# Mixer A's value phase: the sums of a group's weight blocks tied behind the last group's end, and the first rotary tables behind the last sums

## The chip, the cores and the metric

The kernel runs on one core of one Trainium2 chip. A core has TensorE (PE in the profile, with PEld for its weight loads), VectorE (DVE), ScalarE (ACT), GpSimd (POOL) and SyncE (SP), which run side by side and wait for one another by semaphores, and 16 DMA engines. The metric is the device time of one execution in microseconds (us), the median of several.

## The reference

A two-layer encoder over 512 positions of width 1024 in fp32. Layer 0 mixes its tokens with mixer A, layer 1 with mixer B (latent attention), and each mixer is followed by a squared-ReLU MLP. The change touches mixer A, which is, shortened:

```python
def dilated_mixer(h, w_qkv, q_gain, k_gain, w_o):
    qkv = (h @ w_qkv).reshape(B, S, 3, N_GROUPS, A_HEADS, A_HEAD_DIM)
    for g, (window, dil) in enumerate(DIL_CONFIGS):      # 3 groups, 8 heads of 128
        q = rope(rms_norm(qkv[:, :, 0, g], q_gain[g]), S)
        k = rope(rms_norm(qkv[:, :, 1, g], k_gain[g]), S)
        v = qkv[:, :, 2, g]
        o, lse = dilated_group(q, k, v, window, dil)
    wts = softmax(stack(lses), axis=0)
    o = wts[0] * outs[0] + wts[1] * outs[1] + wts[2] * outs[2]
    return o.reshape(B, S, A_WIDTH) @ w_o
```

In words: the normed input h (512 x 1024) is projected to queries, keys and values for three dilation groups, queries and keys are normed and rotated, each group attends in its own window, and the three outputs are merged by their softmax denominators and projected by w_o.

## The kernel before, in words

Matmuls run in fp32r, an fp32 form that keeps fewer bits. So each fp32 operand x is split into a high part (ScalarE copies x to fp32r, "whi" for weights) and a low part (VectorE subtracts it from x, "wlo"), and a product is three matmuls: high by high, high by low, low by high. TensorE waits for both parts, so behind every weight block stand one ScalarE and one VectorE instruction.

The value phase (`v_phase`) computes the values of heads 0 to 5 of each group g = 0, 1, 2 by a block scheme with seven products in place of eight. Rows of h are in two halves, and the weight of a group is cut in 2 x 2 blocks b11, b12, b21, b22 of 512 x 384 that SyncE's queue loads into a ring of six buffers ("wq"). The products are numbered as in the code, and run in the order 2, 1, 5, 3, 6, 7, 4. Products 2, 1, 3 take blocks themselves; 5 takes bT = b11 + b12; 6 takes bT after + b22; 4 takes it after + b21 as well; 7 takes b3 = b12 + b22. All of these sums are VectorE's, two instructions of 128 x 768 each (`add_block`, L349, which shows as "bT<-b,b", "bT<-bT,b" and, for b3, "b<-b,b"). Each product's weights are split in two parts (L421 ScalarE, L422 VectorE; "whi" and "wlo" are rings of four buffers, so a split must wait until TensorE has done with the block four splits back), then 24 matmuls of 384 columns go to each of two PSUM banks (L436). `put` adds a product into the output: the first product of a chain is copied by ScalarE (L453), a later one added or subtracted by VectorE (L455, "vo<-vo,sc"), whereupon TensorE may write the next product of that chain. Chain "a" holds products 1, 6, 7 and 4 in the two banks "sc", so TensorE begins product 7 in a bank when VectorE's subtraction of product 6 has read it.

The first rotary tables (`tables`, L271 and L274, four VectorE instructions) multiply cosines and sines with the gains of group 0's queries and keys. Before, they sit in group 1 behind the put "add".

Behind the value phase come, for four pairs of heads (b = 0 to 3), the query and key projections ("acc<-whi,hT", "acc<-wlo,hT", L191), scores ("sc<-qkT", L591 to L602), the merge of the groups (two small matmuls "scm", L657 and L682, with a chain of small VectorE work between and the scaling of all P, L688, behind), and the products of P with the values (`pv`): transposes of P (L125), copies to pT (L698 VectorE, L705 ScalarE), matmuls L712 and L716 into "sco", and the copy to oT (L718). In the last block there is no next projection, and the output projection ("acc<-whi,hT" with 512 columns) of the heads that are done is mixed in.

The order on each engine is set by a scheduler that lists the instructions by a timeline that it works out itself, over all engines at once. `tc.issue_after(x)` makes what is written under it be listed only behind instruction x. In this change both ends of every tie are VectorE instructions, so the order of VectorE's list keeps it.

Of the kernel before, what the change touches and what calls it, by code (L numbers as in the profile page):

```python
# [10 lines left out]
F32 = mybir.dt.float32  # L11
# [3 lines left out]
ALU = mybir.AluOpType  # L15
# [8 lines left out]
NG = 3  # L24
# [64 lines left out]
def encoder_kernel(ctx: ExitStack, tc: tile.TileContext, x, norm_mix, norm_ffn, a_w_qkv, a_q_gain, a_k_gain,  # L89
# [3 lines left out]
    V, A, G, PE = nc.vector, nc.scalar, nc.gpsimd, nc.tensor  # L93
    uid = [0]
    marks = {}

    def nm(s):
        uid[0] += 1
        return f"{s}_{uid[0]}"
# [167 lines left out]
    def tables(g, gqk, cos, sin):  # L267

        for t in range(2):
            gb = gqk[:, t].rearrange("p (f d) -> p f d", f=2).unsqueeze(1).broadcast_to([P, NT, 2, 64])  # L270
            V.tensor_tensor(cosg[g][:, :, t].rearrange("p r (f d) -> p r f d", f=2),  # L271
                            cos.rearrange("p (r d) -> p r d", r=NT).unsqueeze(2).broadcast_to([P, NT, 2, 64]), gb,
                            op=ALU.mult)
            V.tensor_tensor(sing[g][:, :, t].rearrange("p r (f d) -> p r f d", f=2),  # L274
                            sin.rearrange("p (r f d) -> p r f d", r=NT, f=2), gb, op=ALU.mult)
# [46 lines left out]
    def v_phase(vp):  # L322
# [17 lines left out]
        def block(g, ki, ni, name):  # L340
            t = vp.tile([P, 4, VH], F32, tag="wq", name=nm(name), bufs=6)
            for u in range(2):
                nc.sync.dma_start(t[:, 2 * u:2 * u + 2], wblk(g, ki, ni, u))
            return t

        def add_block(t, x, y):
            for u in range(2):
                us = slice(2 * u, 2 * u + 2)
                V.tensor_tensor(t[:, us], x[:, us], y[:, us], op=ALU.add)  # L349

        def load_x(r):
            for hf in range(2):
# [2 lines left out]
        b11, b21, bT, b12, b22 = {}, {}, {}, {}, {}  # L355
# [62 lines left out]
        def split_w(x):  # L418
            hi = wp.tile([P, 2, 512], F32R, tag="whi", name=nm("whi"))[:, :, :VH]
            lo = wp.tile([P, 2, 512], F32R, tag="wlo", name=nm("wlo"))[:, :, :VH]  # L420
            A.activation(hi, x, AF.Copy)  # L421
            V.tensor_tensor(lo, x, hi.bitcast(F32), op=ALU.subtract)  # L422
            return hi, lo

        def split(p, w, u):
            parts[p, u] = split_w(w[:, 2 * u:2 * u + 2])

        def product(p, w, banks, first, u, t):
            if (p, u) not in parts:
                split(p, w, u)  # L430
            hi, lo = parts[p, u]
            for j in range(2):
                k = 2 * u + j
                ah, al = A_OF[p](k, 0, t), A_OF[p](k, 1, t)
                for i_, (lt, rt) in enumerate(((ah, hi), (ah, lo), (al, hi))):
                    PE.matmul(banks[t][:, :VH], lhsT=lt, rhs=rt[:, j], start=(first and k == 0 and i_ == 0),  # L436
                              stop=(k == 3 and i_ == 2), skip_group_check=True)

        def both(p, w, banks, first):
            for u, t in ((0, 0), (0, 1), (1, 0), (1, 1)):  # L440
                product(p, w, banks, first, u, t)

        def new_banks(chain):
            pl, tg = {"a": (sc_p, "sc"), "b": (tp_p, "tp"), "d": (acc_p, "acc")}[chain]
            return [pl.tile([P, 512], F32, tag=tg, name=nm(tg)) for _ in range(2)]

        def put(g, i, n, how, banks, last):

            o = vo[:, 2 * i + n]
            for t in range(2):  # L450
                acc = banks[t][:, :VH]
                if how == "set":
                    A.activation(o[:, t], acc, AF.Copy)  # L453
                else:
                    marks["put"] = V.tensor_tensor(o[:, t], o[:, t], acc,  # L455
                                                   op=ALU.add if how == "add" else ALU.subtract).ins
                if last:

                    nc.gpsimd.dma_start(vall[g].rearrange("(m r) d -> m r d", r=NT)
                                        [:, 2 * i + t, VH * n:VH * n + VH], o[:, t])  # L460

        def piece(g, ba):

            bb = new_banks("b")
            both(5, bT[g], bb, True)
            put(g, 1, 1, "set", bb, False)
            add_block(bT[g], bT[g], b22[g])
            both(3, b22[g], bb, False)
            put(g, 0, 1, "set", bb, False)
            b3 = vp.tile([P, 4, VH], F32, tag="h32", name=nm("b3"))  # L470
            add_block(b3, b12[g], b22[g])
            both(6, bT[g], ba, False)
            put(g, 0, 1, "sub", ba, True)
            add_block(bT[g], bT[g], b21[g])
            both(7, b3, ba, False)
            put(g, 1, 1, "sub", ba, True)
            both(4, bT[g], ba, False)
            put(g, 1, 0, "set", ba, True)

        def sum_tile():  # L480
            return vp.tile([P, 4, VH], F32, tag="wq", name=nm("bT"), bufs=6)
# [44 lines left out]
        for i in range(2):  # L526
            split_s(2, dif[:, 1, i], i)
        piece(0, ba)

        rot = vp.tile([P, D], F32, tag="xn", name="rot", bufs=2)  # L530
        nc.sync.dma_start(rot[:, 0:C_M1 - C_KEEP], consts[:, C_KEEP:C_M1])
        g0 = rot[:, 768:1024].rearrange("p (t d) -> p t d", t=2)
        load_gains(0, g0)
        for g in range(1, NG):
            b21[g] = block(g, 1, 0, "b21")
            b11[g] = block(g, 0, 0, "b11")
            b12[g] = block(g, 0, 1, "b12")
            b22[g] = block(g, 1, 1, "b22")
            bT[g] = sum_tile()
            parts = {}  # L540
            bd, ba = new_banks("d"), new_banks("a")
            both(2, b21[g], bd, True)
            put(g, 0, 0, "set", bd, False)
            both(1, b11[g], ba, True)
            put(g, 0, 0, "add", ba, True)
            if g == 1:

                with tc.issue_after(marks["put"]):
                    tables(0, g0, rot[:, 0:256], rot[:, 256:768])
            add_block(bT[g], b11[g], b12[g])  # L550
            piece(g, ba)

    ap0 = tc.tile_pool(name="ap0", bufs=1, reuse_waits="tile")
    a0 = ap0.__enter__()
    cosg, sing = ([a0.tile([P, NT, 2, DH], F32, name=n)] for n in ("cosg0", "sing0"))
    with tc.tile_pool(name="vph", bufs=1, reuse_waits="tile") as vp:
        v_phase(vp)
# [701 lines left out]
```

## Time and profile before

| | us |
|---|---|
| median of 3 runs | 1404.27 |
| lowest and highest | 1403.55, 1405.62 |
| profiled execution | 1403.76 |
| its span, first to last instruction | 1402.0 |
| TensorE busy | 1371.6 |
| VectorE busy | 940.0 |
| ScalarE busy | 801.0 |
| GpSimd busy | 224.0 |

The span is what the trace covers; the profiled execution's own time is 1.8 us longer. TensorE's mean granted clock is 0.999. In the trace the value phase's first matmul of L436 stands at 11.1 us and its last at 123.9 us, and the transposes of P run from 236.7 to 497.5 us. A pause of TensorE shows in brackets behind the instruction that follows it, with the instruction that ended it.

### The profile page before, as it was taken

To read this page: it belongs to the slowest core of one execution; us is meant where nothing else is said; L and a number is where in the kernel's file an instruction comes from. 1 tells how busy PE (TensorE), PEld (TensorE's weight loads), DVE (VectorE), ACT (ScalarE), POOL (GpSimd) and SP (SyncE) were. 2 spreads that over 40 slices of the span, in tenths; PEclk is the share of its full clock that TensorE was granted. 3 is DMA by queue.
4 is the path that set the end of the run, shared out by engine and by line. 5 is a ranking of instruction groups with operands and counts; after the bars stand their busy time and mean duration, and the time that the engine had idled before them with its cause. 6 is when DMAs were issued, how large, how long until landed. Compare 5 with 4: busy or idle time off the path is not lost.

```text
span 1402.0 us, 18979 instructions
## 1 busy us (share of the span) xinstructions
PE 1371.6 (98%) x6852; PEld 1163.6 (83%) x6852; DVE 940.0 (67%) x1498; ACT 801.0 (57%) x1643; POOL 224.0 (16%) x240
## 2 busy tenths in 40 slices
PE   7999999999999999999999999999999999999998
PEld 6999887888889989888888878777769888888887
DVE  6886777787788744464655768788745465574747
ACT  6544778687786624453536455777534553644543
POOL 1110212121122001020200204433201020020101
PEclk9999999999999999999999999999999999999999
DMA  9535553655555539486583944211116668493835
GB/s 309 170 134 163 134 130 97 164 131 125 143 130 120 158 106 271 135 186 174 123 237 87 234 96 95 61 31 31 46 46 189 172 131 230 98 234 119 198 88 120
DMA packets 171774, 197.83 MB, mean 141 GB/s; under 512 B 59104, under 2 KB 109024, under 8 KB 171680
## 3 DMA queue, kind: packets, MB, share of 16 engines
q1 hardware_dynamic: 152496, 157.55, 37.7%
q0 software_dynamic: 19184, 39.07, 15.5%
q8 instruction: 54, 0.88, 0.3%
q14 instruction: 40, 0.33, 0.1%
HBM read 176.13 MB, written 7.86 MB: 131 GB/s over the span
## 4 chain that ended last, share of the span: by engine, by line
PE 80%; DVE 7%; DMA 4%; issue 4%; ACT 3%; POOL 1%; SPq 0%; ACTq 0%; DVEq 0%; POOLq 0%
PE acc L191 49%; PE sc L877 9%; PE tp L877 6%; PE sc L436 3%; PE tp L125 2%; DMA wqs<-in_ffn_w_dram 2%; PE acc L1170 1%; DVE wlo L820 1%; PE sc L1064 1%; DMA xT<-t 1%; PE acc L1146 1%; PE tp L436 1%; PE sc L602 1%; PE sco L716 1%; PE sco L712 1%
## 5 line engine op out<-in xcount | busy, mean ns | idle before, releaser
L191 PE MATMUL acc<-whi,hT 128*128 128x512 f32 (+2 forms) x1208 | 377.2, 388 | 1.9 <-ACT hT L761 1.0
L191 PE MATMUL acc<-hT_f,whi 128*128 128x512 f32 (+1 forms) x1152 | 317.5, 366 | 0.0
L159 DVE TENSOR_TENSOR wlo<-raw,whi 128x1024 fp32r<-128x1024 f32 (+3 forms) x146 | 172.8, 1188 | 169.3 <-ACT whi L158 168.8
L191 PEld LDWEIGHTS acc<-whi,hT 128*128 128x128 f32 x1208 | 224.4, 188 | 42.7 <-ACT hT L761 1.7
L158 ACT ACTIVATE whi<-raw 128x1024 fp32r<-128x1024 f32 (+3 forms) x146 | 149.7, 1029 | 159.6 <-PE acc L191 74.8
L191 PEld LDWEIGHTS acc<-hT_f,whi 128*128 128x128 f32 x1152 | 207.9, 189 | 34.9
L191 PE MATMUL acc<-wlo,hT 128*128 128x512 f32 (+2 forms) x604 | 232.9, 386 | 0.4 <-DVE wlo L159 0.4
L820 DVE TENSOR_TENSOR wlo<-wqs,whi 128x1024 fp32r<-128x1024 f32 x112 | 137.7, 1231 | 114.0 <-ACT whi L819 113.9
L819 ACT ACTIVATE whi<-wqs 128x1024 fp32r<-128x1024 f32 x112 | 118.3, 1060 | 162.0 <-PE acc L191 66.2
L191 PE MATMUL acc<-hT_f,wlo 128*128 128x512 f32 (+1 forms) x576 | 204.1, 366 | 0.0
L877 PE MATMUL sc<-whi,asp 128*128 128x512 f32 x512 | 165.1, 390 | 1.0 <-DVE resid L851 1.0
L805 POOL DMA_DIRECT2D wqs<-in_ffn_w_dram x64 | 77.7, 1347 | 539.7 <-DVE wlo L820 358.1
L191 PEld LDWEIGHTS acc<-wlo,hT 128*128 128x128 f32 x604 | 113.7, 188 | 20.1 <-DVE wlo L159 1.0
L191 PEld LDWEIGHTS acc<-hT_f,wlo 128*128 128x128 f32 x576 | 108.3, 189 | 17.3
L877 PEld LDWEIGHTS sc<-whi,asp 128*128 128x128 f32 x512 | 96.2, 188 | 21.6 <-issue 1.8
L877 PE MATMUL tp<-whi,asp 128*128 128x512 f32 x352 | 112.1, 390 | 0.9 <-DVE resid L851 0.9
L133 POOL TENSOR_TENSOR qrs<-rs_v,nhalf 128x4 f32<-128x4 f32 x48 | 64.6, 1348 | 265.0 <-DVE rs_v L130 241.8
L877 PE MATMUL sc<-wlo,asp 128*128 128x512 f32 x256 | 99.7, 390 | 0.0
L307 ACT ACTIVATE qkT<-xT 128x1024 uint16<-128x1024 uint16 x48 | 56.5, 1181 | 39.5 <-DMA xT<-t 39.4
L877 PEld LDWEIGHTS tp<-whi,asp 128*128 128x128 f32 x352 | 66.1, 188 | 15.0 <-DVE resid L851 1.3
L877 PE MATMUL tp<-wlo,asp 128*128 128x512 f32 x176 | 68.2, 390 | 0.0
L138 ACT ACTIVATE junk<-acc 128x128 f32<-128x128 f32 x192 | 52.3, 273 | 12.3 <-PE acc L191 8.7
(236 smaller groups left out, 2186.8 us busy)
## 6 DMA issues: line engine op xcount, KB each, us to landing
wqs<-in_ffn_w_dram SPq DMA_DIRECT2D x80, 512.0 KB, 5.0
raw<-in_ffn_w_dram SPq DMA_DIRECT2D x64, 512.0 KB, 4.6
wqs<-in_ffn_w_dram POOLq DMA_DIRECT2D x64, 512.0 KB, 7.2
raw<-in_a_w_qkv_dram SPq DMA_DIRECT2D x96, 256.0 KB, 3.2
b<-in_a_w_qkv_dram SPq DMA_DIRECT2D x24, 384.0 KB, 5.7
vall<-vo POOLq DMA_DIRECT2D x24, 192.0 KB, 2.3
raw<-in_a_w_o_dram SPq DMA_DIRECT2D x8, 512.0 KB, 4.1
raw<-in_b_w_o_dram SPq DMA_DIRECT2D x8, 512.0 KB, 3.8
```

What stands on the lines that cost most here:

```text
L125: return PE.transpose(o, i, ident)
L133: G.tensor_tensor(out, v[:, :n], nhalf[:, :n], op=ALU.pow)
L138: A.activation(junk, x, AF.Square, scale=1.0 / math.sqrt(dim), accum_out=out)
L158: A.activation(hi[:, :nk, :n], raw[:, :nk, :n], AF.Copy)
L159: V.tensor_tensor(lo[:, :nk, :n], raw[:, :nk, :n], hi[:, :nk, :n].bitcast(F32), op=ALU.subtract)
L191: last = PE.matmul(accs[o][:, oc], lhsT=lt, rhs=rt, start=(kt == 0 and p_i == 0 and hv == 0), stop=(kt == total - 1 and p_i == 2), skip_gr ...
L307: A.activation(dst, xT.rearrange("p (h c) t -> p c t h", h=2), AF.Copy)
L436: PE.matmul(banks[t][:, :VH], lhsT=lt, rhs=rt[:, j], start=(first and k == 0 and i_ == 0), stop=(k == 3 and i_ == 2), skip_group_check=True)
L805: marks["sum"] = nc.gpsimd.dma_start(t, src, accum_op=ALU.add).ins
L819: A.activation(hi, x, AF.Copy)
L820: V.tensor_tensor(lo, x, hi.bitcast(F32), op=ALU.subtract)
L877: PE.matmul(bk[t], lhsT=lt, rhs=rt[:, j], start=(first and k == 0 and i_ == 0), stop=(k == 3 and i_ == 2), skip_group_check=True)
```

## The change

`add_block` returns its last instruction, and the splits and puts are marked, so that others can be tied behind them. For groups 1 and 2, the first sums (bT = b11 + b12) are issued after the last group's second subtraction of product 7 ("minus") and after the last split of product 2; the sums b3 are issued after the sums bT + b22. The first rotary tables are issued after the sums bT + b21 of the last group. No computation is added or taken away. Line numbers in the changed kernel are one higher behind `add_block`, and five higher behind `v_phase`.

```diff
--- before.py
+++ after.py
@@ -346,7 +346,8 @@
         def add_block(t, x, y):
             for u in range(2):
                 us = slice(2 * u, 2 * u + 2)
-                V.tensor_tensor(t[:, us], x[:, us], y[:, us], op=ALU.add)
+                last = V.tensor_tensor(t[:, us], x[:, us], y[:, us], op=ALU.add)
+            return last.ins
 
         def load_x(r):
             for hf in range(2):
@@ -419,7 +420,7 @@
             hi = wp.tile([P, 2, 512], F32R, tag="whi", name=nm("whi"))[:, :, :VH]
             lo = wp.tile([P, 2, 512], F32R, tag="wlo", name=nm("wlo"))[:, :, :VH]
             A.activation(hi, x, AF.Copy)
-            V.tensor_tensor(lo, x, hi.bitcast(F32), op=ALU.subtract)
+            marks["split"] = V.tensor_tensor(lo, x, hi.bitcast(F32), op=ALU.subtract).ins
             return hi, lo
 
         def split(p, w, u):
@@ -464,16 +465,20 @@
             bb = new_banks("b")
             both(5, bT[g], bb, True)
             put(g, 1, 1, "set", bb, False)
-            add_block(bT[g], bT[g], b22[g])
+            after_t = add_block(bT[g], bT[g], b22[g])
             both(3, b22[g], bb, False)
             put(g, 0, 1, "set", bb, False)
             b3 = vp.tile([P, 4, VH], F32, tag="h32", name=nm("b3"))
-            add_block(b3, b12[g], b22[g])
+            with ExitStack() as behind:
+                if g:
+                    behind.enter_context(tc.issue_after(after_t))
+                add_block(b3, b12[g], b22[g])
             both(6, bT[g], ba, False)
             put(g, 0, 1, "sub", ba, True)
-            add_block(bT[g], bT[g], b21[g])
+            marks["sums", g] = add_block(bT[g], bT[g], b21[g])
             both(7, b3, ba, False)
             put(g, 1, 1, "sub", ba, True)
+            marks["minus", g] = marks["put"]
             both(4, bT[g], ba, False)
             put(g, 1, 0, "set", ba, True)
 
@@ -540,15 +545,15 @@
             parts = {}
             bd, ba = new_banks("d"), new_banks("a")
             both(2, b21[g], bd, True)
+            seconds = marks["split"]
             put(g, 0, 0, "set", bd, False)
             both(1, b11[g], ba, True)
             put(g, 0, 0, "add", ba, True)
-            if g == 1:
-
-                with tc.issue_after(marks["put"]):
-                    tables(0, g0, rot[:, 0:256], rot[:, 256:768])
-            add_block(bT[g], b11[g], b12[g])
+            with tc.issue_after(marks["minus", g - 1]), tc.issue_after(seconds):
+                add_block(bT[g], b11[g], b12[g])
             piece(g, ba)
+        with tc.issue_after(marks["sums", NG - 1]):
+            tables(0, g0, rot[:, 0:256], rot[:, 256:768])
 
     ap0 = tc.tile_pool(name="ap0", bufs=1, reuse_waits="tile")
     a0 = ap0.__enter__()
```

The scheduler lists everything up to the end of mixer A anew. Three places, before and after; digits behind a name are buffer numbers.

The first is VectorE's list at the end of group 0, where products 6 and 7 of that group end (splits "wlo", subtractions "vo") and the sums bT_671 and b_110 of group 1 stand. Before:

```order
L422 TENSOR_TENSOR wlo_584<-b_70_542,whi_583 128x2x384
L455 TENSOR_TENSOR vo<-vo,sc_154 128x384
L349 TENSOR_TENSOR bT_671<-b_84_662,b_85_665 128x768 x2
L422 TENSOR_TENSOR wlo_600<-b_70_542,whi_599 128x2x384
L422 TENSOR_TENSOR wlo_620<-bT_384,whi_619 128x2x384
L455 TENSOR_TENSOR vo<-vo,sc_155 128x384
L422 TENSOR_TENSOR wlo_636<-bT_384,whi_635 128x2x384
L349 TENSOR_TENSOR b_110_824<-b_85_665,b_86_668 128x768 x2
L455 TENSOR_TENSOR vo<-vo,sc_154 128x384
L422 TENSOR_TENSOR wlo_677<-b_83_659,whi_676 128x2x384
L455 TENSOR_TENSOR vo<-vo,sc_155 128x384
L422 TENSOR_TENSOR wlo_693<-b_83_659,whi_692 128x2x384
```

Now:

```order
L423 TENSOR_TENSOR wlo_584<-b_70_542,whi_583 128x2x384
L456 TENSOR_TENSOR vo<-vo,sc_154 128x384
L423 TENSOR_TENSOR wlo_600<-b_70_542,whi_599 128x2x384
L423 TENSOR_TENSOR wlo_620<-bT_384,whi_619 128x2x384
L456 TENSOR_TENSOR vo<-vo,sc_155 128x384
L423 TENSOR_TENSOR wlo_636<-bT_384,whi_635 128x2x384
L456 TENSOR_TENSOR vo<-vo,sc_154 128x384
L423 TENSOR_TENSOR wlo_677<-b_83_659,whi_676 128x2x384
L456 TENSOR_TENSOR vo<-vo,sc_155 128x384
L423 TENSOR_TENSOR wlo_693<-b_83_659,whi_692 128x2x384
L349 TENSOR_TENSOR bT_671<-b_84_662,b_85_665 128x768 x2
L423 TENSOR_TENSOR wlo_711<-b_84_662,whi_710 128x2x384
```

The two pairs of sums have left the place among group 0's splits and subtractions; bT_671 stands behind the two splits of group 1's product 2 (wlo_677, wlo_693).

The second is TensorE's list at the second head of the first pair (b = 0), between the products of P with groups 1 and 2 and those with group 0 ("sc_2352" are the next pair's scores). Before:

```order
L712 MATMUL sco_2311<-pT_2295,vt_1454 128x128
L591 MATMUL sc_2352<-qkT_1990 128x128
L595 MATMUL sc_2352<-qkT_1990 128x128
L591 MATMUL sc_2352<-qkT_1990 128x128
L716 MATMUL sco_2311<-pT_2302,v0n_1455 128x4x32
```

Now (the 17 projection matmuls are counted in these rows and in those just behind the last one shown, up to the v0n product):

```order
L717 MATMUL sco_2311<-pT_2295,vt_1454 128x128
L596 MATMUL sc_2352<-qkT_1990 128x128
L600 MATMUL sc_2352<-qkT_1990 128x128
L596 MATMUL sc_2352<-qkT_1990 128x128
L600 MATMUL sc_2352<-qkT_1990 128x128
L191 MATMUL acc_2631<-wlo_2707,hT_91 128x512
L191 MATMUL acc_2631<-whi_2706,hT_91 128x512 x2
L191 MATMUL acc_2631<-wlo_2707,hT_91 128x512
L191 MATMUL acc_2631<-whi_2706,hT_91 128x512
L191 MATMUL acc_2632<-whi_2699,hT_91 128x512
L191 MATMUL acc_2632<-wlo_2700,hT_91 128x512
```

Before, one more score matmul apart, nothing stands between the scores and the product with pT_2302; now 17 projection matmuls do.

The third is TensorE's list in the last block, at the second small matmul of its merge (scm_4645). Before:

```order
L191 MATMUL acc_4864<-wlo_4874,hT_4802 128x512
L682 MATMUL scm_4645<-ca,xsel_4621 128x4 x2
L125 MATMUL tp_4815<-ck,P_4083 128x128 x4
L125 MATMUL tp_4822<-ck,P_4085 128x128 x4
L191 MATMUL acc_4861<-whi_4873,hT_4802 128x512 x2
L191 MATMUL acc_4861<-wlo_4874,hT_4802 128x512
L191 MATMUL acc_4862<-whi_4873,hT_4802 128x512 x2
L191 MATMUL acc_4862<-wlo_4874,hT_4802 128x512
```

Now:

```order
L191 MATMUL acc_4864<-whi_4879,hT_4802 128x512 x2
L191 MATMUL acc_4864<-wlo_4880,hT_4802 128x512
L191 MATMUL acc_4864<-whi_4879,hT_4802 128x512
L687 MATMUL scm_4645<-ca,xsel_4621 128x4 x2
L125 MATMUL tp_4815<-ck,P_4083 128x128 x4
L125 MATMUL tp_4822<-ck,P_4085 128x128 x4
L717 MATMUL sco_4843<-pT_4820,vt_4090 128x128
L125 MATMUL tp_4829<-ck,P_4081 128x128 x4
L125 MATMUL tp_4836<-ck,P_4081 128x128 x4
```

The projection matmuls behind the transposes tp_4815 and tp_4822, 40 of them up to the end of the first head, now all stand ahead of scm_4645. VectorE's list at the same place, before:

```order
L159 TENSOR_TENSOR wlo_5028<-raw_5025,whi_5027 128x1024
L683 COPY me_4632<-scm_4645 128x8
L159 TENSOR_TENSOR wlo_5066<-raw_5063,whi_5065 128x1024
L698 COPY pT_4820<-tp_4815 128x512
L698 COPY pT_4827<-tp_4822 128x512
L688 TENSOR_TENSOR P_4081<-P_4081,me_4632 128x1024
L688 TENSOR_TENSOR P_4082<-P_4082,me_4632 128x1024
L159 TENSOR_TENSOR wlo_5072<-raw_5069,whi_5071 128x1024
```

Now:

```order
L693 TENSOR_TENSOR P_4086<-P_4086,me_4632 128x512
L159 TENSOR_TENSOR wlo_5072<-raw_5069,whi_5071 128x1024
L688 COPY me_4632<-scm_4645 128x8
L703 COPY pT_4820<-tp_4815 128x512
L159 TENSOR_TENSOR wlo_5078<-raw_5075,whi_5077 128x1024
L693 TENSOR_TENSOR P_4081<-P_4081,me_4632 128x1024
L693 TENSOR_TENSOR P_4082<-P_4082,me_4632 128x1024
L703 COPY pT_4827<-tp_4822 128x512
```

Behind the copy from scm_4645, the splits wlo_5072 and wlo_5078 have come forward (wlo_5066 has gone ahead), and pT_4827 is behind both P.

## The prediction

> **What bounds the kernel now.** I read the page's first part, then a table of windows, then the waits at the value phase's matmul line, then single instructions on TensorE and VectorE. First the page's busy row and four of the windows (columns: the window, its length, and then busy time and instructions of PE, PEld, DVE, ACT, POOL, the granted clock, DMA share, GB/s).
>
> ```profile
> PE 1371.6 (98%) x6852; PEld 1163.6 (83%) x6852; DVE 940.0 (67%) x1498; ACT 801.0 (57%) x1643; POOL 224.0 (16%) x240
> ...
> 9.00:62.00 53.00, 51.39 (x285) 48.86 (x286) 49.46 (x68) 34.77 (x58) 7.16 (x12) 1.00 0.78 247
> 62.00:92.00 30.00, 29.38 (x170) 29.09 (x169) 24.98 (x33) 15.25 (x22) 4.35 (x9) 1.00 0.54 185
> 92.00:124.00 32.00, 32.00 (x185) 31.78 (x184) 21.43 (x27) 16.80 (x24) 5.01 (x10) 1.00 0.22 74
> 240.00:280.00 40.00, 37.71 (x223) 32.59 (x222) 30.40 (x54) 26.24 (x69) 6.29 (x6) 1.00 0.60 144
> 480.00:512.00 32.00, 30.40 (x183) 26.22 (x182) 17.38 (x23) 7.63 (x10) 0.00 (x0) 1.00 0.45 150
> ```
>
> TensorE is the bound everywhere: 1371.6 of 1402.0 us. The change adds and removes no matmul, so it can only move TensorE's pauses. The value phase, whose groups 1 and 2 it edits, lies between about 9 and 124 us, and in its last window TensorE does not pause at all. VectorE there is dense before 62 us (49.46 of 53) and has slack later. The waits at the phase's matmul line say who holds TensorE up (us, times):
>
> ```profile
>   DVE vo L455: 2.0, 5
>   DVE wlo L422: 1.6, 2
> ```
>
> So at most 3.6 us in the whole phase are VectorE's, part of it in group 0's start, which the change leaves alone. Where they lie is seen in VectorE's timeline at the end of group 0, and TensorE's beside it (start, duration, instruction, idle before it and its releaser):
>
> ```profile
> 52.49 0.54 DVE L455 TENSOR_TENSOR vo<-vo,sc 128x384 f32<-128x384 f32 x1
> 52.95 1.81 DVE L349 TENSOR_TENSOR bT<-b,b 128x768 f32<-128x768 f32 x2
> 54.69 0.95 DVE L422 TENSOR_TENSOR wlo<-b,whi 128x768 fp32r<-128x768 f32 x1
> 57.76 1.81 DVE L349 TENSOR_TENSOR b<-b,b 128x768 f32<-128x768 f32 x2
> 59.50 0.54 DVE L455 TENSOR_TENSOR vo<-vo,sc 128x384 f32<-128x384 f32 x1
> ```
>
> ```profile
> 54.54 0.51 PE L436 MATMUL sc<-whi,Ssp 128*128 128x384 f32 x2
> 55.69 0.45 PE L436 MATMUL sc<-wlo,Ssp 128*128 128x384 f32 x1 [0.64 <-DVE wlo L422]
> ...
> 56.50 0.34 PE L436 MATMUL sc<-whi,Ssp 128*128 128x384 f32 x1
> 57.02 0.44 PE L436 MATMUL sc<-whi,Ssp 128*128 128x384 f32 x1 [0.19 <-DVE vo L455]
> ...
> 59.27 0.62 PE L436 MATMUL acc<-whi,hT 128*128 128x384 f32 x2
> 60.09 0.44 PE L436 MATMUL sc<-whi,hT 128*128 128x384 f32 x1 [0.21 <-DVE vo L455]
> ```
>
> The brackets count from a modelled end that overlaps the next matmul, so I price a pause from start to start. Back to back, a 384-column matmul takes 0.17 us (32.00 us for 185 instructions between 92 and 124 us). Then the three pauses are 0.81 (55.69 less 54.54 less two matmuls), 0.35 and 0.47. All three stand behind sums of group 1: the weight split that TensorE needs at 55.69 starts at 54.69 because two sums (1.74 us, 52.95 to 54.69) ran first, and the subtraction of 59.50 starts when the next two sums end.
>
> **The change part by part.** *Boundary of groups 0 and 1.* The first sums of group 1 now issue only after group 0's last subtraction, the second pair after the bT sums. Both pairs leave the place just shown; the instructions behind them (splits and subtractions) move up by 1.74 us each time, more than any of the three pauses. Gain 0.81 + 0.35 + 0.47 = 1.6 us; 0 is the other end, if TensorE then waits for ScalarE's half of the split instead. The sums come again behind the second split of product 2, where before VectorE has this room:
>
> ```profile
> 65.12 0.96 DVE L422 TENSOR_TENSOR wlo<-b,whi 128x768 fp32r<-128x768 f32 x1 [2.88 <-ACT whi L421]
> ...
> 73.45 0.68 DVE L271 TENSOR_TENSOR cosg<-rot 128x512 f32<-128x512 f32 x1
> ...
> 112.61 0.96 DVE L422 TENSOR_TENSOR wlo<-b,whi 128x768 fp32r<-128x768 f32 x1 [2.69 <-ACT whi L421]
> ```
>
> 2.88 us idle, and 1.74 us of sums go into it, so they cost nothing there; without that cover they would cost the 0.8 of one pause. *Tables.* Four operations of 0.68 us leave 73.45 us and stand behind the last sums, in the idle time that ends at 112.61 (2.69 us for 2.4 us of work at a 0.60 us step). Their first reader is the query and key evacuation after 124 us. Cost 0, gain 0: TensorE did not pause at 73.45. *Group 1 into 2.* One pause stands there:
>
> ```profile
> 84.66 0.34 PE L436 MATMUL sc<-whi,Ssp 128*128 128x384 f32 x1
> 85.63 0.41 PE L436 MATMUL sc<-whi,Ssp 128*128 128x384 f32 x1 [0.62 <-DVE vo L455]
> ```
>
> 0.97 - 0.17 = 0.8 us. The sums ahead of that subtraction go, but in the new order three splits are queued ahead of it, the last of which must wait until ScalarE has a weight buffer back from TensorE. Between -0.8 and 0; I take -0.2. *Group 2's same place.* It did not pause. Now its subtractions stand behind two more splits than before, so between 0 and the 0.8 of group 1's case; I take +0.6. Value phase: -1.6 - 0.2 + 0.6 = **-1.2 us**. The blocks' loads are issued when their buffers come free, a few us later for one block, and are read some 20 us on: 0.
>
> *What is re-listed behind it.* The edit also makes the scheduler list the rest of mixer A anew, so pauses there can go or come. Before, the first head pair (b = 0) has three:
>
> ```profile
> 246.32 0.83 PE L712 MATMUL sco<-pT,vt 128*128 128x128 f32 x6
> 247.53 1.06 PE L125 MATMUL tp<-ck,P 128*128 128x128 f32 x8 [0.37 <-DVE P L688]
> 248.42 0.83 PE L712 MATMUL sco<-pT,vt 128*128 128x128 f32 x6
> 249.70 0.50 PE L191 MATMUL acc<-wlo,hT 128*128 128x512 f32 x1 [0.44 <-DVE wlo L159]
> ...
> 265.77 0.39 PE L591 MATMUL sc<-qkT 128*128 128x128 f32 x2
> 267.63 0.49 PE L716 MATMUL sco<-pT,v0n 128*128 128x128 f32 x2 [1.47 <-ACT pT L705]
> ```
>
> From start to start, with 0.11 us for a 128-column matmul, 0.54, 0.61 and 1.64 us. In the new order 17 projection matmuls stand ahead of the last one (17 x 0.227 = 3.9 us, more than 1.64), where none stood; and VectorE scales P and makes the second split earlier. So -2.8; 0 is the other end, if ScalarE's copies come late by as much again, since they are queued behind the transposed queries' DMA. A later pair loses such a fill of 12 matmuls. The pair between has none before or after and does not pause, so I count 0 (up to +1.6 by the 1.64).
>
> The last block goes the other way. Its rows before, TensorE and then VectorE:
>
> ```profile
> 480.53 1.07 PE L125 MATMUL tp<-ck,P 128*128 128x128 f32 x8
> ...
> 496.32 0.39 PE L712 MATMUL sco<-pT,vt 128*128 128x128 f32 x2
> 497.23 0.66 PE L125 MATMUL tp<-ck,P 128*128 128x128 f32 x4 [0.52 <-ACT pT L705]
> ...
> 503.28 0.71 PE L191 MATMUL acc<-whi,hT 128*128 128x512 f32 x2
> 504.97 0.50 PE L191 MATMUL acc<-whi,hT 128*128 128x512 f32 x1 [0.98 <-ACT hT L761]
> ```
>
> ```profile
> 246.16 2.35 DVE L688 TENSOR_TENSOR P<-P,me 128x1024 f32<-128x1024 f32 x2
> ...
> 494.69 1.22 DVE L159 TENSOR_TENSOR wlo<-raw,whi 128x1024 fp32r<-128x1024 f32 x1
> 495.82 0.68 DVE L718 COPY oT<-sco 128x512 f32<-128x512 f32 x1
> 496.43 0.68 DVE L698 COPY pT<-tp 128x512 f32<-128x512 f32 x1
> ```
>
> Pauses 0.7 and 1.2, together 1.9 us. Before, 40 output-projection matmuls (9 us) stand behind the small matmul scm of the merge and fill TensorE while VectorE works off its queue. In the new order all of them stand ahead of scm and none behind. Behind scm VectorE's queue is then bare: with steps of 1.13 (split), 1.14 (a P) and 0.61 (copy), TensorE waits about 0.6 for the first pT (a split is ahead of it), 2.0 for P of the third transpose (copy, split, P: 2.9 us, less the 0.9 of eight transposes), 1.2 for the buffer that the second pT copy frees behind both P, 0.5 for pT behind oT, and again 1.2 at the end: 5.5, against 1.9. **+3.6 us**, between 0, if the 13.6 us now ahead of scm let the queue be done before, and +6.9, below.
>
> Sum: -1.2 - 2.8 + 3.6 = -0.4 us. The profiled execution took 1403.76 us (span 1402.0), 0.5 below the median of 1404.27; on the median that is **1403.9 us**, no change that can be told: a measurement here tells about 0.2%, 2.8 us.
>
> A rule speaks against the tail. First its row:
>
> ```profile
> 8.91 1.97 PE L125 MATMUL tp<-ck,xn 128*128 128x128 f32 x8 [8.91 <-DVE xn L376]
> ```
>
> After 8.91 us idle, eight transposes take 1.97 us, against 1.07 at 480.53, although the granted clock shows 1.00 in every window. That lasts until about 14.3 us, where matmuls are back at 0.17. The Trainium skill, TensorE: Matmul & The Clock Gate, Part 1, has TensorE at half its clock after an idle window of about 3.4 us, until as long a busy one; the trace agrees after that start, and no pause of 2 us or less in this trace shows it. By that rule a tail with 5.5 us of pauses among few matmuls might fall back too.
>
> **The rivals.** *Faster.* The tail costs nothing new, since with 13.6 us of matmuls ahead of scm VectorE and ScalarE come there with empty queues: -1.2 - 2.8 = -4.0, 1400.3 us. For it: VectorE is busy 17.38 of 32 us between 480 and 512. Against it: both P of group 0 need scm's own result, and cannot be done ahead. Chance 0.22. *Slower.* VectorE's queue behind scm runs through bare: two splits, two copies and two P are 2.3 + 1.2 + 2.3 = 5.8 us, the second head's copies add 1.8 and the end 1.2, 8.8 against 1.9: +6.9, in all +2.9, 1407.2 us. The tail eats the gains from the point where its pauses pass 1.9 + 4.0 = 5.9 us, and is seen as a loss from 5.9 + 2.8 = 8.7. For it: a strict queue with splits for later weights between. Against it: TensorE has transposes and products of its own between the steps, some 4 us. Chance 0.16. *The clock falls back in the tail.* At the start 5.4 us (8.91 to 14.3) ran at half speed and cost 2.7; as much behind scm gives 1403.9 + 2.7 = 1406.6. Against it: no single pause above comes near 3 us. Chance 0.03. *The edit does not do what it says:* splits wait for ScalarE instead, and the value phase gains nothing: -2.8 + 3.6 = +0.8, 1405.1. Against it: ScalarE is busy 34.77 of 53 us there. Chance 0.08.
>
> **How the numbers follow.** My case has 0.51: 1403.9, by itself 1402 to 1406. Faster by over 0.2% is the first rival, 0.22; slower is the second and a third of the clock's, 0.17; the rest, 0.61, is within. Each case spreads by about 1 us for the places I count at 0. The range runs from just inside the first rival's 1400.3 to just inside the second's 1407.2: 1400.8 to 1407.0 leaves about 2 in 10 outside.
>
> **What would show it.** Step one: in the changed trace no pause for wlo or vo at the end of group 0, and about 0.6 each at the subtractions between products 6 and 7 of groups 1 and 2. Step two: no pause before the second head's v0n product of b = 0. Step three: behind the second scm of the last block three or four pauses, the longest near 2 us and for P on VectorE. The sum is wrong if the tail's pauses stay near 2 us or pass 8.7, or if new pauses over 1 us stand between 124 and 480 us.

## The result, and the profile after

The changed kernel is slower: 1411.36 us median of six runs (1410.08 to 1412.41) against 1404.55 us (1403.55 to 1405.62) for the kernel before, a ratio of 1.0048 with a 95% interval of 1.0035 to 1.0061. I had forecast 1403.9 us and no change. The profiled execution took 1412.16 us, its span is 1410.4 us.

First the page's busy row and the windows of the changed kernel (columns as before: window, length, busy time and instructions of PE, PEld, DVE, ACT, POOL, granted clock, DMA share, GB/s).

```profile
PE 1375.2 (98%) x6852; PEld 1166.3 (83%) x6852; DVE 942.0 (67%) x1498; ACT 801.4 (57%) x1643; POOL 229.5 (16%) x240
...
9.00:62.00 53.00, 52.19 (x290) 51.09 (x291) 47.55 (x66) 35.80 (x59) 7.39 (x12) 1.00 0.79 249
92.00:124.00 32.00, 31.45 (x180) 30.98 (x179) 26.18 (x34) 16.68 (x23) 4.76 (x9) 1.00 0.21 73
240.00:280.00 40.00, 39.28 (x232) 34.20 (x232) 33.56 (x63) 29.28 (x81) 13.87 (x7) 1.00 0.54 145
480.00:520.00 40.00, 34.89 (x188) 29.77 (x187) 21.33 (x37) 10.05 (x23) 0.00 (x0) 0.91 0.38 126
```

Up to 62 us TensorE is busier than before, and from 240 to 280 as well: what the prediction wanted to see there is there. The loss shows in the last window: 5 us without TensorE's work, and a granted clock of 0.91, where every window of before had 1.00. Finer windows of the same place:

```profile
484.00:490.00 6.00, 6.00 (x28) 4.95 (x28) 4.21 (x12) 0.48 (x1) 0.00 (x0) 1.00 0.40 97
490.00:495.00 5.00, 2.56 (x18) 2.01 (x16) 3.79 (x5) 1.64 (x2) 0.00 (x0) 1.00 0.75 256
495.00:502.00 7.00, 5.70 (x26) 5.33 (x27) 2.20 (x3) 1.19 (x2) 0.00 (x0) 0.52 0.92 329
502.00:510.00 8.00, 7.71 (x58) 7.14 (x57) 2.67 (x4) 1.71 (x3) 0.00 (x0) 0.99 0.11 42
```

TensorE works half of the five microseconds behind 490, and from 495 to 502 it runs at about half speed. TensorE's instructions behind the second small matmul of the last merge (at 490.64), and VectorE's there:

```profile
491.00 1.07 PE L125 MATMUL tp<-ck,P 128*128 128x128 f32 x8
492.57 0.49 PE L717 MATMUL sco<-pT,vt 128*128 128x128 f32 x2 [0.50 <-DVE pT L703]
495.61 1.09 PE L125 MATMUL tp<-ck,P 128*128 128x128 f32 x4 [2.56 <-DVE P L693]
497.39 1.11 PE L125 MATMUL tp<-ck,P 128*128 128x128 f32 x4 [0.69 <-ACT pT L710]
498.30 3.19 PE L717 MATMUL sco<-pT,vt 128*128 128x128 f32 x14
501.28 0.63 PE L721 MATMUL sco<-pT,v0n 128*128 128x128 f32 x2
501.71 0.83 PE L125 MATMUL tp<-ck,P 128*128 128x128 f32 x4
502.38 0.39 PE L721 MATMUL sco<-pT,v0c 128*128 128x128 f32 x2
```

```profile
491.83 0.68 DVE L703 COPY pT<-tp 128x512 f32<-128x512 f32 x1
493.11 1.23 DVE L159 TENSOR_TENSOR wlo<-raw,whi 128x1024 fp32r<-128x1024 f32 x1 [0.59 <-ACT whi L158]
494.25 2.35 DVE L693 TENSOR_TENSOR P<-P,me 128x1024 f32<-128x1024 f32 x2
496.52 0.69 DVE L703 COPY pT<-tp 128x512 f32<-128x512 f32 x1
```

This is the queue of the prediction: a copy, a split for a later weight, both P, a copy. TensorE pauses three times beside it, the longest for 2.72 us. Four transposes take 1.09 us where eight took 1.07 at 491.00.

Elsewhere, the waits of TensorE between 124 and 480 us of the changed kernel (us in total, times, longest):

```profile
PE sc L607 <- ACT qkT L307: 1.9, 3, 1.0
PE acc L191 <- ACT vt L635: 0.8, 1, 0.8
PE acc L191 <- DVE rs_v L130: 0.7, 1, 0.7
PE sc L596 <- ACT qkT L307: 0.6, 1, 0.6
```

The three pauses of the first pair are gone, but scores now wait for queries, which before cost half a microsecond in all of that stretch. A ledger of the two profiled executions, with pauses over 0.25 us from start to start:

| place | before, us | changed, us | difference |
|---|---|---|---|
| first matmul of the program | 8.91 | 9.51 | +0.6 |
| value phase from 50 us on | 0.81 + 0.35 + 0.37 + 0.79 = 2.3 | 0.62 + 0.72 = 1.3 | -1.0 |
| 124 to 480 us | 3.6 | 5.7 | +2.1 |
| last block behind its second scm | 0.69 + 1.15 + 0.26 = 2.1 | 0.67 + 2.72 + 1.00 + 0.45 + 1.15 + 0.26 = 6.25 | +4.2 |
| matmuls at half speed (28 from 495.61 to 502.38: 6.77 less the 1.00 of pause, less 28 x 0.11) | 0 | 2.7 | +2.7 |

The sum is 8.6; the spans differ by 8.4. The first row is not the change's: over the ten traces the wait at the start lies between 8.4 and 9.8 us. The third row is not sharp either. Of its 5.7 us, 1.21 is one wait of scores for queries at 186 us. With the list of before, four of the kernels below (e1, e5, e6, e7) show 0.82 to 1.07 us four score matmuls ahead of that place, while the trace of before and e8 show none. Taken whole, the stretch has 3.1 to 4.2 us of pauses in before, e1, e5, e7 and e8, and about 5.7 in the changed kernel, e3 and e4.

### The profile page after: what moved, and what is told of

Read it like the earlier page. It is cut to its first block, busy times and chain, and to the rows that moved or that the text cites. A ratio compares the mean times of both kernels' runs of the same rounds, so it can differ in the third digit from the quotient of the medians.

```text
span 1410.4 us, 18987 instructions
## 1 busy us (share of the span) xinstructions
PE 1375.2 (98%) x6852; PEld 1166.3 (83%) x6852; DVE 942.0 (67%) x1498; ACT 801.4 (57%) x1643; POOL 229.5 (16%) x240
## 4 chain that ended last, share of the span: by engine, by line
PE 80%; DVE 7%; ACT 5%; DMA 5%; issue 3%; SPq 0%; ACTq 0%; DVEq 0%
PE acc L191 44%; PE sc L882 10%; PE tp L882 7%; DMA xT<-t 3%; PE tp L125 3%; PE sc L437 3%; PE tp L437 1%; PE acc L1175 1%; PE sc L1069 1%; DVE wlo L825 1%; PE acc L1151 1%; PE sco L717 1%; PE sco L721 1%; PE acc L437 1%; ACT t L299 1%
## 5 line engine op out<-in xcount | busy, mean ns | idle before, releaser
L133 POOL TENSOR_TENSOR qrs<-rs_v,nhalf 128x4 f32<-128x4 f32 x48 | 71.0, 1483 | 261.2 <-DVE rs_v L130 228.3
L307 ACT ACTIVATE qkT<-xT 128x1024 uint16<-128x1024 uint16 x48 | 56.6, 1180 | 38.4 <-DMA xT<-t 38.2
```

The lines of the kernel that those rows point to most:

```text
L133: G.tensor_tensor(out, v[:, :n], nhalf[:, :n], op=ALU.pow)
L307: A.activation(dst, xT.rearrange("p (h c) t -> p c t h", h=2), AF.Copy)
```

## The experiments

Two theories after the result: A, the loss is in the re-listed last block, where the fill left its place behind scm; B, the ties themselves delay sums in the value phase. A third, C, looks at the queries' waits in the middle. What makes them separable is that the three parts of the change act on the lists differently. With only the first sums tied, TensorE's and ScalarE's lists are those of before, instruction for instruction, from end to end. With only the b3 sums tied, all lists behind the value phase are those of the changed kernel.

**The first sums alone** (e1): the b3 tie and the tables' move are undone.

```diff
-            with ExitStack() as behind:
-                if g:
-                    behind.enter_context(tc.issue_after(after_t))
-                add_block(b3, b12[g], b22[g])
+            add_block(b3, b12[g], b22[g])
...
+            if g == 1:
+                with tc.issue_after(marks["put"]):
+                    tables(0, g0, rot[:, 0:256], rot[:, 256:768])
```

> Only the first sums (bT = b11 + b12) of groups 1 and 2 are tied behind the last group's end; the b3 sums and the tables stay where they were before. TensorE's and ScalarE's lists are then those of before, instruction for instruction, and VectorE's differs in the value phase alone. Theory A (the loss is in the re-listed last block, where the projection matmuls left the place behind the merge's second small matmul): no loss, the pauses of 0.81 and 0.35 us at the end of group 0 go, the tail keeps its 2 us of pauses; 1402.5 to 1403.8 us against 1404.5. Theory B (the loss comes from the ties themselves, sums that arrive late in groups 1 and 2): most of the +6.8 us stays, 1408 or more. Theory C (the loss comes from the middle, where scores wait for queries): no loss either, since the middle's list is unchanged; A and C part in the third run.

Measured: 1405.04 us against 1404.95, ratio 1.0001 (0.9992 to 1.0010). B falls for the first sums: their tie does not cost what the change costs. But the gain expected did not come either. In the value phase one wait is left, and it has grown:

```profile
85.95 0.41 PE L437 MATMUL sc<-whi,Ssp 128*128 128x384 f32 x1 [1.78 <-DVE vo L456]
```

VectorE's timeline there shows the next group's b3 sums, which have come into the place that the first sums left:

```profile
82.65 1.83 DVE L349 TENSOR_TENSOR b<-b,b 128x768 f32<-128x768 f32 x2
84.39 0.95 DVE L423 TENSOR_TENSOR wlo<-bT,whi 128x768 fp32r<-128x768 f32 x1
85.26 1.01 DVE L456 TENSOR_TENSOR vo<-vo,sc 128x384 f32<-128x384 f32 x2
```

So 1.5 us are won at the end of group 0, and the pause between products 6 and 7 of group 1 grows from 0.79 to 1.95 us.

**The b3 sums alone** (e2): the first sums go back to their place behind the put "add", the tables too; the tie of b3 stays.

```diff
-            with tc.issue_after(marks["minus", g - 1]), tc.issue_after(seconds):
-                add_block(bT[g], b11[g], b12[g])
+            add_block(bT[g], b11[g], b12[g])
```

> Only the b3 sums are tied behind the sums bT + b22; the first sums and the tables stay where they were before. Behind the value phase all three lists are then those of the changed kernel. Theory A: the last block's pauses (about 6 us and matmuls at half speed) and the middle's stay as in the changed kernel, while the 0.81 and 0.35 us at the end of group 0 come back: 1411.5 to 1413 us. Theory B with the first sums as the cause: about 1404.5.

Measured: 1416.03 us, ratio 1.0081 (1.0067 to 1.0094), even above the changed kernel and 3 us above the top of what theory A gave. Its waits in the value phase and in the tail:

```profile
PE sc L437 <- DVE vo L456: 2.6, 3, 2.0
...
PE tp L125 <- DVE P L694: 1.9, 1, 1.9
```

The tail is listed as in the changed kernel and pauses much like it (0.66, 2.04 and 0.86 us at its first three places), with a clock of 0.72 from 496 to 508 us. The value phase has lost too (2.14 us between products 6 and 7 of group 1, where the changed kernel has 0.62): 3.9 us of pauses there against 2.3 before. So the loss comes with the b3 tie, and all but about 1.6 us of it lies behind the value phase, where that tie only sets a listing.

**The fill put back behind scm** (e3): the changed kernel, and 36 of the 60 projection matmuls of the last block tied behind the second scm.

```diff
+                        if tie is not None and gi == 0 and 2 * u + j == 3:
+                            behind.enter_context(tc.issue_after(tie))
...
+                    if tie is not None and gi == 0 and u == 2:
+                        behind.enter_context(tc.issue_after(tie))
```

> The changed kernel, with 36 of the last block's 60 projection matmuls tied behind the second small matmul of its merge; everything ahead of the last block is as in the changed kernel. Theory A: the tail falls back to about 2 us of pauses at full clock, so -6.8 us: 1404 to 1406 us, with the middle's +2.1 and the value phase's -1.4 left. Theory C: the tail is not the place, 1409 to 1411.4 us.

Measured: 1410.96 us, ratio 1.0048 (1.0035 to 1.0060), nothing won. I had expected 1404 to 1406. The pauses behind scm went, as the fill stands there again, but one of their size came ahead of it, and the clock fell in that one (a row of TensorE, and two windows):

```profile
485.31 0.98 PE L691 MATMUL scm<-ca,xsel 128*128 128x4 f32 x4 [3.31 <-DVE xsel L686]
```

```profile
481.00:485.00 4.00, 1.00 (x5) 0.50 (x3) 3.19 (x11) 1.74 (x6) 0.00 (x0) 0.93 0.37 104
485.00:492.00 7.00, 6.69 (x19) 5.54 (x20) 5.21 (x9) 0.00 (x0) 0.00 (x0) 0.55 0.49 167
```

The time is the one that theory C gave, but the trace has the loss in the last block still. So theory A was half right: here the fill's place decides only where the pause lies. What is late is the whole chain of the last merge, and the lateness is set ahead of it, at the last scores. The last score matmuls of mixer A, before and then in the changed kernel:

```profile
464.86 1.95 PE L602 MATMUL sc<-qkT 128*128 128x128 f32 x16
```

```profile
474.17 0.71 PE L607 MATMUL sc<-qkT 128*128 128x128 f32 x4
```

From the last of them to the end of the pause for hT (L761 before) it is 505.0 - 466.5 = 38.4 us before, 513.3 - 474.6 = 38.7 in the changed kernel and 511.9 - 474.0 = 37.9 in e3. That these are alike does not show a chain of a fixed length: before, 223 matmuls fill that stretch but for 1.8 us of pauses, while the changed kernel has 187 matmuls there, 6.0 us of pauses and 2.7 us of half speed, and e4 below, at full clock, takes 35.7 us. What the traces do show is that the changed kernel comes to the last merge 8 us later, with 36 matmuls (6.6 us) of the work beside it done ahead. Theory A2: the changed listing has the products of the pair b = 2 (which end at 441 us, before at 449) ahead of the second half of the last query and key projection, whose last matmul is at 450 instead of 447; its four blocks then come to VectorE in a bunch, and one of them waits until a transposing transfer has read a buffer ("t"), here in the changed kernel:

```profile
462.11 0.76 DVE L291 TENSOR_TENSOR t<-acc,sing 128x256 f32<-128x256 f32 x2 [1.55 <-DMA xT<-t]
```

**The last queries late, in the kernel before** (e6): the value phase and everything up to the pair b = 2 as before; 36 matmuls of the last projection tied behind that pair's products.

```diff
+                    if tie is not None and gi == 1 and i >= 2:
+                        behind.enter_context(tc.issue_after(tie))
...
+                                tie=marks["pv"] if (b, g) == (3, 2) else None):
```

> The kernel before, with 36 of the 96 matmuls of the last query and key projection (b = 3, third group) tied behind the products of the pair ahead (b = 2), as the changed kernel has them listed. Everything ahead of that place is as before, the value phase too. Theory A2 (the last block runs bare since its last scores come late, because the last projection was listed behind the pair's products): last scores 6 to 9 us later than the 464.9 us of before, behind the second scm no projection matmuls, pauses of 5 to 6 us with a stretch at about half clock: 1410 to 1413 us. Rival (the tail's loss hangs on something of the value phase's change): 1405 to 1407 us, with what the 36 matmuls' own place costs.

Measured: 1412.59 us against 1404.15, ratio 1.0060 (1.0047 to 1.0074). Its last scores and its tail:

```profile
472.72 0.60 PE L605 MATMUL sc<-qkT 128*128 128x128 f32 x4
...
492.58 0.49 PE L715 MATMUL sco<-pT,vt 128*128 128x128 f32 x2 [0.50 <-DVE pT L701]
494.94 0.63 PE L125 MATMUL tp<-ck,P 128*128 128x128 f32 x4 [1.87 <-DVE P L691]
496.59 0.92 PE L125 MATMUL tp<-ck,P 128*128 128x128 f32 x4 [1.02 <-DVE pT L701]
```

The last score matmul is 6.5 us late (473.05 against 466.53), the scheduler itself then lists all 60 projection matmuls ahead of scm, and a tail like that of the changed kernel stands there, with pauses of 0.67, 2.03 and 1.18 us, in a kernel that has none of the change. A2 holds as far as late last scores are enough for such a tail; the value phase is not needed for it. It is not a copy of the changed kernel: here the last projection ends at 455 us, there at 450.

**The fill ahead of scm, scores on time** (e7): the kernel before, its last scm tied behind all 60 projection matmuls.

```diff
+            if ahead is not None:
+                ahead()
+                behind.enter_context(tc.issue_after(marks["fill"]))
             ps2 = sc_p.tile([P, 512], F32, tag="sc", name=nm("scm"))
```

> The kernel before, with the last block's second scm tied behind all 60 projection matmuls, and nothing else changed; the last scores stay on time. Theory of the prediction (the fill's place behind scm decides): pauses of 5 to 6 us behind scm, in all 1409 to 1413 us. Rival (lateness of the last scores decides, and the fill's place follows from it): scm itself is ready 9 us ahead, so the splits and copies on VectorE and ScalarE are done by then and the tail pauses 2 to 4 us: 1405 to 1407 us.

Measured: 1406.98 us, ratio 1.0019 (1.0010 to 1.0028). Here the scheduler lists the first eight transposes ahead of scm as well, so that their copies are done ahead, and TensorE has one long wait, 1.62 us from start to start, and two of 0.41 and 0.45 behind it:

```profile
494.02 1.06 PE L125 MATMUL tp<-ck,P 128*128 128x128 f32 x8 [1.45 <-DVE P L694]
```

The fill's place with the scores on time costs 2.8 us (by its interval 1.4 to 3.9; the last block's pauses in the two traces differ by 1.8), a third of what e6 costs, and the clock stays at 1.00. With the transposes behind scm it could cost more; that was not tried.

**The tail kept busy** (e4): the changed kernel, with 20 transposes that nobody reads in the long pause.

```diff
+            if (b, h) == (HA // 2 - 1, 0):
+                for _ in range(20):
+                    transpose(marks["ps2"][:, 128:256], Pt[1][0][:, 0])
```

> The changed kernel with 20 transposes more that nobody reads (20 x 0.109 = 2.2 us of TensorE), put into the pause of 2.72 us of the last block. They change no list otherwise. If the half-speed matmuls behind the pauses (495.6 to 501.8 us) come of TensorE's own idleness, they stay at full speed: 1411.4 - 2.6 = 1408.8 us, with a granted clock of 1.00 in the tail, and of the pauses what the 20 transposes do not fill. If the slow stretch has another cause (the transfers of that time, 0.9 to 1.0 of the DMA engines), the time stays at 1411 to 1412 and the clock at about 0.5 for some 6 us.

Measured: 1409.35 us against 1404.95, ratio 1.0033 (1.0020 to 1.0046), where the changed kernel had 1.0048: about 2 us less, by more work. The transposes, and below them the window from 495 to 502 us as above:

```profile
492.86 2.40 PE L125 MATMUL scm<-ck,P 128*128 128x128 f32 x20
```

```profile
495.00:502.00 7.00, 5.57 (x49) 5.17 (x48) 3.51 (x4) 1.19 (x2) 0.00 (x0) 1.00 0.91 345
```

The DMA engines are as busy as in the changed kernel (0.91, there 0.92), and the clock is full. So the slow stretch came of TensorE's idleness, not of the transfers. The changed kernel and this one were timed on different occasions and their intervals overlap; the clock column is what decides.

**First sums and tables, b3 untied** (e5).

```diff
-                if g:
-                    behind.enter_context(tc.issue_after(after_t))
                 add_block(b3, b12[g], b22[g])
```

> The first sums tied as in the change and the tables behind the last sums, but the b3 sums left untied. TensorE's list behind the value phase is then that of before, and in group 1 VectorE's first subtraction of product 6 stands ahead of the last two splits, where the first run (first sums alone) had it behind them, with a pause of 1.95 us. Theory A2 (behind the value phase only the listing counts, and the listing follows the b3 tie): no pause at the end of group 0 and none or up to 0.6 us between products 6 and 7 of group 1, downstream as before: 1404.95 - 1.5 to 2.3 = 1402.6 to 1403.5 us. Rival (moving the tables also costs, by its later place): 1405 or more.

Measured: 1402.38 us against 1404.15, ratio 0.9987 (0.9978 to 0.9996): 1.8 us less (by the interval 0.6 to 3.1), inside the 1.5 to 2.3 expected, and faster than both kernels. TensorE's only wait between 50 and 124 us is

```profile
PE sc L437 <- DVE vo L456: 0.2, 1, 0.2
```

With the tables out of group 1, VectorE comes to the subtraction of product 6 ahead of the last two splits. Behind the value phase TensorE pauses at the places of before, and once more at 183 us (0.86), as in e1, e6 and e7. This is the value phase's gain that the change was able to give, without the other listing.

**Tables alone** (e8): only the tables move.

```diff
-            if g == 1:
-                with tc.issue_after(marks["put"]):
-                    tables(0, g0, rot[:, 0:256], rot[:, 256:768])
...
+        with tc.issue_after(marks["sums", NG - 1]):
+            tables(0, g0, rot[:, 0:256], rot[:, 256:768])
```

> Only the first tables move behind the last sums; the sums stay untied. TensorE's list behind the value phase is that of before. Theory A2: the pauses of 0.81, 0.35 and 0.37 us at the end of group 0 stay, nothing else changes: 1404 to 1405.5 us. Rival (the tables' move is what costs): above 1406 us.

Measured: 1404.29 us against 1404.15, ratio 1.0000 (0.9991 to 1.0009). In the time, the tables cost and bring nothing that can be told by themselves. In the trace something else does change. TensorE's waits between 50 and 124 us, before and then here:

```profile
PE sc L436 <- DVE vo L455: 1.0, 3, 0.6
PE sc L436 <- DVE wlo L422: 0.6, 1, 0.6
```

```profile
PE sc L437 <- DVE wlo L423: 0.6, 1, 0.6
PE sc L437 <- DVE vo L456: 0.4, 2, 0.2
```

The pauses at the end of group 0 stay, as expected, but the one of 0.79 us between products 6 and 7 of group 1 is gone: there, too, the subtraction now stands ahead of the last two splits. So the gain of e5 has two parts, the 1.5 us of the first sums and the pause of group 1, which goes with the tables.

## Why the prediction was wrong, step by step

The value phase was right to a few tenths. Forecast -1.6 at the end of group 0, -0.2 in group 1, +0.6 in group 2; the trace has -1.5, -0.2 (0.79 to 0.62) and +0.7 (0 to 0.72). Three readings there were off, without weight for the sum. The third pause is 0.37 us, counted from the matmul right ahead of it, not 0.47. The 3.6 us of waits at the line count idle time before weight loads together with that before matmuls; before matmuls alone it is 1.6. And the tables were put at "gain 0": by e8 their move alone takes group 1's pause away, so the -0.2, a choice between -0.8 and 0, was in part luck.

The first pair was right as far as it went: its three pauses (2.8 us) are gone. The step that failed is the one that set the rest of the middle at nothing ("the places I count at 0"): between 124 and 480 us the changed kernel has scores that wait for queries (0.79, 0.28, 1.21, 0.34, 0.90), 0.88 us in a projection, and 0.98 and 0.28 just ahead of the last scores. That is 5.7 us, where before had 0.8 besides the first pair's, so 4.9 us are new; 1.21 us is a pause of the kind that the prediction named as a sign of a wrong sum. They lie in the same re-listing that took the others away, and I had looked for what goes, not for what comes. The net is +2.1 in place of -2.8. That these come of the listing is borne out by e2, e3 and e4, which have the same list there and nearly the same pauses at the same matmuls, while the kernels with the list of before have about 2 us less. No run changes the middle's list alone, so this is argued and not shown, and about 1 us of it may be chance, as said at the ledger. Which rule of the scheduler put the queries so late was not tried.

The second step that failed is the tail's, which was right in its pauses and too small by its clock. Step by step, forecast and measured: first pT 0.6 and 0.67, P 2.0 and 2.72, the second buffer 1.2 and 1.00, pT behind oT 0.5 and 0.45, the end 1.2 and 1.15. The one that is off has a split whose high half came 0.59 us late from ScalarE. The clock was a rival with a chance of 0.03, priced at 2.7 us; 2.7 is what the trace shows, and about 2 what e4 gives. That the price fits is luck, for it was taken from 5.4 us at the program's start, while the slow stretch here lasts nearly 7 us with a pause of 1.00 in it. The reason for the low chance, that "no single pause above comes near 3 us", was the wrong test. Between 491.9 and 495.6 TensorE ran two matmuls of 0.11 us in 3.7 us, and behind that it was slow. The two rivals were also not separate: the tail that I forecast was the one that lets the clock fall, so its price belonged into the sum.

The prediction's picture of the tail was half of its cause. It read the fill's place behind scm as what decides. e7 prices that at 2.8 us, and e3 shows that putting the fill back wins nothing; the rest is the last scores' lateness, which is set some 75 rows and more ahead of the second scm in TensorE's list, and which I did not compare.

The rival that the edit does not do what it says was wrong for the changed kernel. For the first sums alone (e1) its result came true, a value phase that gains nothing, and its reason in part: in group 1 one split waited 0.94 us for ScalarE, and the b3 sums (1.74 us) behind it made the subtraction later still.

## What to carry to other kernels

Where a scheduler lists a program by a timeline of its own, an edit that wins 1 us at its place can lose 8 elsewhere: compare the two lists to the end, and above all how far ahead of the last dependent chain its first link stands, since a chain that starts late cannot be filled from behind. Try the parts of such a change one by one: here a part that looked harmless (the b3 tie) brought the other listing, and the other two without it gave the gain. A tail that is worked out to pause for several microseconds with little work between is to be priced with the clock's fall, too.

## What the runs showed of the hardware

Short pauses with little work between were as bad as one long one. The clock fell in the changed kernel with pauses of 0.67 and 2.72 us and 0.2 us of work between, in e6 with 0.67, 2.03 and 1.18 us and 0.2 and 0.4 us of work between, and in e3 in one pause of 3.3 us. It stayed at 1.00 in e7 (1.62 us, and 0.41 behind it) and e4 (0.91 and 0.85). The Trainium skill, TensorE: Matmul & The Clock Gate, Part 1, speaks of an idle window of about 3.4 us. The changed kernel agrees with it if the window counts activity and not one unbroken pause, which these runs suggest and do not prove. In e3 the clock fell sooner than that: of the 4 us from 481 TensorE is busy for the first 1.00, and a mean clock of 0.93 leaves about 0.5 us at half speed, so it fell some 2.5 us into the pause. That no pause reaches 3 us is thus no safe sign.

In the changed kernel the slow stretch lasted from 495 to about 502 us. Its price was 2.7 us for 3.4 us of pause, and 2.2 us of useless transposes took it away.
